# A third accumulator for the in-projection, from the scan's idle PSUM banks, and an earlier release of held-back loads

## The chip, the cores and the metric

One NeuronCore of a Trainium2 chip runs the whole kernel in one launch. The metric is the device time of a launch in microseconds, the median over several executions. The engines that matter are TensorE (PE in the rows), VectorE (DVE), ScalarE (ACT) and SyncE (SP), whose queue issues all the weight loads.

## What is computed

The block is a pre-norm hybrid decoder layer on 256 tokens of width 2048. Cut to what matters here:

```python
h = rms_norm(x, g1) * (1 + scale1) + shift1        # scale, shift, gate: columns of c @ w_mod
u, k, q, v, gates = split(h @ w_in)                # 2048 x 8192: 4 x 1024 columns and 2 x 2048
y_attn = moba_attention(rotary(norm(q)), rotary(norm(k)), v)
y_ssm  = s5_branch(u)                              # a diagonal scan over the 256 tokens
x = x + gate1 * (merge(y_attn, y_ssm, sigmoid(gates)) @ w_out)
x = x + gate2 * conv_ffn(rms_norm(x, g2) * (1 + scale2) + shift2)
```

## The kernel before

**Weights.** Every weight tile is 512 KB (128 partitions of 1024 floats). SP loads it into a ring of five `raw` buffers; ACT rounds it into `whi` (line 213, three buffers), DVE subtracts into `wlo` (line 218, three buffers), and PE makes three products, activations split the same way. A `raw` slot is free again when its `wlo` is made. Modulation weights go through the same ring: tiles of `w_m` go straight to PE as `modp` (line 491), and the `raw` slot is free when those four products are done; tiles of `w_g` go to DVE (line 529), which reduces them there. `load_ahead` issues loads in the order of a list, `order`, as far as the ring has room; modulation loads are held back in `behind_weights` until two more weight tiles have been issued (`LAG`).

**The first stage.** The in-projection is made in five chunks of its 16 k-tiles (2, 2, 4, 4, 4). In each chunk the blocks u (2), k (2), q (2), v (2) and one early gate block `gep` (two in chunk 0) each get a partial sum; in the last chunk the order is u, k, gates, q, v. Between chunks a partial sum lives in SBUF. So from chunk 1 on each block begins with a seed, an ACT copy from SBUF into the PSUM accumulator (line 287 for `up`, 366 for `kp`, `qp`, `vp`, four copies at line 285 for the gates), and ends with an ACT copy back (line 1079, or 1136 for gates) that is written one weight tile later. The accumulators alternate between two PSUM buffers of two banks each (`mm_tile`). Two more banks (`bu_tile`) are for the scan, which begins in the last chunk, when u is finished.

**Order.** The program is written in one order by the planner, and the tile framework schedules each engine's instructions from it; each engine then runs its own list in order, waiting for semaphores. Beside the projections, pieces of other work are woven in: the modulation of the next chunk, the scan's set-up, the scan itself (`zp`, `zt`, `kp` of `cpad`, `bu`, `py`), the norms and rotations of k and q, and transposes `qt`. After the chunks come the rest of the gates (`gsp`), the attention, the branch projections and the feed-forward part, which is some three quarters of the time.

Of the kernel before, what the change touches and what calls it, by code (L numbers as in the profile page):

```python
# [42 lines left out]
def block_kernel(ctx: ExitStack, tc: tile.TileContext, I, out):  # L43
# [11 lines left out]
    def mm_tile(shape, name):  # L55
        return ps.tile(shape, F32, name=name, tag="mm", bufs=2)
# [3 lines left out]

    def py_tile(shape, name):
        return ps.tile(shape, F32, name=name, tag="py", bufs=1)

    def m1_tile(shape, name):
        return ps.tile(shape, F32, name=name, tag="m1", bufs=1)
# [22 lines left out]
    def wsrc(w, kb, c0):  # L88
        return w[kb, c0 // 512]
# [15 lines left out]
    place = {"seen": 0}  # L105


    order, behind_weights = [], []
# [7 lines left out]
    def ring_of(i):  # L116
        return "mod" if plan[i][0] == "m" and "mod" in ring else "w"

    def see_next():

        i = place["seen"]
        place["seen"] += 1
        if plan[i][3] and ring_of(i) == "w":
            behind_weights.append([i, plan[i][3]])
            return
        order.append(i)
        if plan[i][0] == "w":
            for entry in behind_weights:
                entry[1] -= 1
            while behind_weights and behind_weights[0][1] <= 0:  # L130
                order.append(behind_weights.pop(0)[0])

    def load_next():
        i = order.pop(0)
        src = plan[i][1]
        r = ring_of(i)
        held[r] += 1
        raw = ring[r]()

        if r == "mod" and "lo" in place:  # L140
            V.tensor_copy(raw[:, 0, 0:1], place["lo"][:, 0, 0:1].bitcast(F32))
        flat = raw.rearrange("p a b -> p (a b)")
        DMA.dma_start(flat, src)
        loaded[i] = (raw, r)
# [9 lines left out]
    def follow(inst):  # L154
        if "mod" in behind:
            after(inst, behind.pop("mod"))
# [5 lines left out]
    def load_ahead():  # L162
        while True:
            while not order and place["seen"] < len(plan):
                see_next()
            if not order:
                break
            r = ring_of(order[0])
            if held[r] >= room[r]:
                break  # L170
            load_next()
# [14 lines left out]
    def later(n, fn):  # L186
        agenda.setdefault(clock["step"] + n, []).append(fn)
# [13 lines left out]
    def take_back(g):  # L201
        bg[:] = [entry for entry in bg if entry[0] is not g]

    def drain(g):
        for _ in g:
            pass
        take_back(g)
# [18 lines left out]
    def add_weights(src, fn):  # L226
        weights.append(len(plan))
        plan.append(("w", src, fn, 0))
# [38 lines left out]
    def chan_block(name, w, c0, kbs, act_hi, act_lo, post, k0=0, w0=None, seed=None, groups=None):  # L267

        st = {}

        def step(u, hi, lo):
            if u == 0:
                if groups:
                    st["m"] = []
                    for make, ms in zip((mm_tile, bu_tile, py_tile), groups):
                        part = make([128, len(ms), 256], name)
                        st["m"] += [part[:, i] for i in range(len(ms))]
                else:
                    st["p"] = mm_tile([128, 4, 256], name)
                    st["m"] = [st["p"][:, m] for m in range(4)]  # L280
                if seed is not None:
                    src = seed()
                    if isinstance(src, list):
                        for m in range(4):
                            A.copy(st["m"][m], src[m])
                    else:
                        A.copy(st["p"].rearrange("p a b -> p (a b)"), src)
            p = st["m"]
            starts = [ms[0] for ms in groups] if groups else (0, 2)
            for m in range(4):  # L290
                ms = slice(128 * m, 128 * m + 128)
                for k in range(2):
                    kk = k0 + 2 * u + k
                    first = u == 0 and k == 0 and seed is None
                    follow(PE.matmul(p[m], hi[:, k, ms], act_hi(kk), start=first and m in starts,
                                     stop=False, skip_group_check=True))
                    PE.matmul(p[m], hi[:, k, ms], act_lo(kk), start=False, stop=False,
                              skip_group_check=True)
                    PE.matmul(p[m], lo[:, k, ms], act_hi(kk), start=False,
                              stop=u == kbs - 1 and k == 1, skip_group_check=True)  # L300
                for ms in groups if groups and u == kbs - 1 else ():
                    if ms[-1] == m:
                        post(p, ms)
            if u == kbs - 1 and not groups:
                later(1, lambda: post(st["p"]))

        for u in range(kbs):
            add_weights(wsrc(w, (w0 if w0 is not None else k0 // 2) + u, c0),
                        lambda hi, lo, u=u: step(u, hi, lo))
# [48 lines left out]
    def tok_block(name, w, c0, kbs, act_hi, act_lo, post, k0=0, seed=None):  # L358

        st = {}  # L360

        def step(u, hi, lo):
            if u == 0:
                st["p"] = mm_tile([128, 2, 512], name)
                if seed is not None:
                    A.copy(st["p"], seed())
            p = st["p"]
            for k in range(2):
                kk = k0 + 2 * u + k
                for t in range(2):  # L370
                    ts = slice(128 * t, 128 * t + 128)
                    follow(PE.matmul(p[:, t], act_hi(kk)[:, ts], hi[:, k],
                                     start=u == 0 and k == 0 and seed is None, stop=False,
                                     skip_group_check=True))
                    PE.matmul(p[:, t], act_hi(kk)[:, ts], lo[:, k], start=False, stop=False,
                              skip_group_check=True)
                    PE.matmul(p[:, t], act_lo(kk)[:, ts], hi[:, k], start=False,
                              stop=(u == kbs - 1 and k == 1), skip_group_check=True)
            if u == kbs - 1:
                later(1, lambda: post(p))  # L380

        for u in range(kbs):
            add_weights(wsrc(w, k0 // 2 + u, c0), lambda hi, lo, u=u: step(u, hi, lo))
# [40 lines left out]
    for i in range(2):  # L424
        p = mm_tile([128, 2, 512], "cb")
# [611 lines left out]
    def all_mods():  # L1037
        while mods:
            next_mod()

    def parts_of(units):
        return sum(len(unit) for unit in units)
# [84 lines left out]
    def sig_post(b, p):  # L1127
        if b % 2 == 0:
            sig_s[b // 2] = e8("sig_s")
        A.activation(sig_s[b // 2][:, 4 * (b % 2):4 * (b % 2) + 4], p, AF.Sigmoid)  # L1130
# [6 lines left out]

    cols = {"u": 3072, "k": 1024, "q": 0, "v": 2048}
    last = len(chunks) - 1
    for c, (k0, nk) in enumerate(chunks):  # L1140
        place["mod"] = 0.0
        if c < last:
            mods += mod1(*chunks[c + 1])
            rate = parts_of(mods) / (4 * nk - 2.0 + nk // 2 * EARLY[c])
        else:
            drain(set_gen)
            mods += mod2(0)
            rate = R_LAST
        for key in "ukgqv" if c == last else "ukqvg":
            for b in range(2 if key != "g" else EARLY[c]):  # L1150
                def add():
                    if key == "g":
                        chan_block("gep", w_in, 6144 + 512 * b, nk // 2, h_hi, h_lo,
                                   lambda p, b=b, c=c: sig_post(b, p) if c == last else keep(b, p), k0=k0,
                                   seed=(lambda b=b: sums[b]) if c else None)
                        return
                    seeded = c > 0
                    (chan_block if key == "u" else tok_block)(
                        key + "p", w_in, cols[key] + 512 * b, nk // 2, h_hi, h_lo,
                        lambda p, key=key, b=b, c=c: gather(key, b, c, p, seeded), k0=k0,  # L1160
                        seed=(lambda key=key, b=b: part(key, b)) if seeded else None)

                with_mods(add, rate)
        all_mods()
        go()
# [278 lines left out]
```

## Time and the profile before

| | |
|---|---|
| median of 3 runs | 1524.7 us (1523.32 to 1530.68) |
| the profiled execution | 1520.47 us, of which 1518.6 us are the span of its instructions |
| mean granted TensorE clock in it | 0.987 of full speed |
| TensorE busy | 96% of the span |
| VectorE, ScalarE busy | 73%, 55% |

The profile gives for each instruction its start, its duration and, in brackets, how long its engine had stood idle before it and who ended that. Busy shares are averages over the whole span, so a single stage is read from a table by stretches of time and from the instructions themselves.

### The profile page before, as it was taken

The numbers are of one execution on the slowest core, as the hardware profiler recorded it, in microseconds if no ns is written. First come the engines' busy times: TensorE is split into PE (matmuls) and PEld (weight loads), VectorE is DVE, ScalarE is ACT, GpSimd is POOL, SyncE is SP. The second block draws the span as 40 slices with busy tenths as digits, with TensorE's granted clock in tenths as the row PEclk, the third lists the DMA queues.
The fourth block names the chain that finished last, engine by engine and source line by source line (L and its number), as shares of the span: only waits on it lengthen the run. The fifth ranks groups of instructions, "written<-read, shape, count | busy, mean of one in ns | idle before, by whom it ended". The sixth has DMA issues, their size and how long they took to land.

```text
span 1518.6 us, 24307 instructions
## 1 busy us (share of the span) xinstructions
PE 1463.7 (96%) x9382; PEld 1237.9 (82%) x9382; DVE 1109.5 (73%) x1881; ACT 842.0 (55%) x1193; POOL 9.8 (1%) x22
## 2 busy tenths in 40 slices
PE   7979999899999999999989999999999999999998
PEld 4657768689977788888868888888888888888887
DVE  3879865886677889998578888886555667766654
ACT  4755767867775534654445555555444455555443
POOL 1000000000000000000000000000000000000000
PEclk9989999999999999999999999999999999999999
DMA  8878888533458887978576777775555555555663
GB/s 322 306 238 307 304 321 296 179 126 126 139 170 298 300 301 276 332 262 315 176 281 235 245 263 262 246 258 191 194 189 188 193 190 186 193 191 186 205 212 107
DMA packets 99109, 353.47 MB, mean 233 GB/s; under 512 B 10961, under 2 KB 13137, under 8 KB 98993
## 3 DMA queue, kind: packets, MB, share of 16 engines
q1 hardware_dynamic: 97808, 348.17, 66.7%
q0 software_dynamic: 1040, 3.61, 0.7%
q8 instruction: 73, 1.20, 0.3%
q14 instruction: 42, 0.34, 0.1%
q10 hardware_dynamic: 146, 0.15, 0.0%
HBM read 349.79 MB, written 2.10 MB: 232 GB/s over the span
## 4 chain that ended last, share of the span: by engine, by line
PE 74%; DVE 10%; DMA 6%; ACT 5%; issue 3%; POOL 0%; SPq 0%; ACTq 0%; DVEq 0%
PE dp L329 11%; PE vp L329 10%; PE gp L329 10%; PE dp L331 6%; PE vp L331 5%; PE gp L331 5%; PE outp L329 4%; DVE wlo L218 4%; ACT whi L213 2%; PE outp L331 2%; PE modp L491 2%; PE ppp L329 2%; PE gap L329 2%; DMA raw<-in_w_m_dram 2%; DMA raw<-in_w_g_dram 2%
## 5 line engine op out<-in xcount | busy, mean ns | idle before, releaser
L218 DVE TENSOR_TENSOR wlo<-raw,whi 128x1024 fp32r<-128x1024 f32 x464 | 566.1, 1222 | 296.6 <-ACT whi L213 294.6
L213 ACT CAST whi<-raw 128x1024 fp32r<-128x1024 f32 x464 | 487.0, 1051 | 521.4 <-PE dp L329 131.8
L329 PE MATMUL vp<-hl,whi 128*128 128x512 f32 x704 | 244.9, 391 | 1.2 <-DVE gate L1307 1.2
L329 PE MATMUL dp<-g,whi 128*128 128x512 f32 x704 | 244.3, 391 | 0.0
L329 PE MATMUL gp<-hl,whi 128*128 128x512 f32 x640 | 222.3, 391 | 0.0
L331 PE MATMUL dp<-g,wlo 128*128 128x256 f32 x704 | 197.7, 281 | 0.0
L331 PE MATMUL vp<-hl,wlo 128*128 128x256 f32 x704 | 197.1, 280 | 0.0
L331 PE MATMUL gp<-hl,wlo 128*128 128x256 f32 x640 | 179.2, 280 | 0.0
L329 PEld LDWEIGHTS vp<-hl,whi 128*128 128x128 f32 x704 | 131.7, 187 | 30.5 <-ACT whi L213 1.5
L329 PEld LDWEIGHTS dp<-g,whi 128*128 128x128 f32 x704 | 131.9, 187 | 28.6
L329 PEld LDWEIGHTS gp<-hl,whi 128*128 128x128 f32 x640 | 119.7, 187 | 26.2
L331 PEld LDWEIGHTS vp<-hl,wlo 128*128 128x128 f32 x704 | 133.1, 189 | 0.0
L331 PEld LDWEIGHTS dp<-g,wlo 128*128 128x128 f32 x704 | 133.0, 189 | 0.0
L331 PEld LDWEIGHTS gp<-hl,wlo 128*128 128x128 f32 x640 | 121.0, 189 | 0.0
L329 PE MATMUL gap<-hl,whi 128*128 128x512 f32 x256 | 92.7, 403 | 0.0
L329 PE MATMUL outp<-m,whi 128*128 128x512 f32 x256 | 90.8, 399 | 0.0
L529 DVE SCALAR_TENSOR_TENSOR raw<-raw,cb 128x1024 f32<-128x1024 f32 x60 | 73.1, 1219 | 22.0 <-DMA raw<-in_w_g_dram 21.5
L529 DVE SCALAR_TENSOR_TENSOR mraw<-mraw,cb 128x1024 f32<-128x1024 f32 x56 | 68.2, 1221 | 17.4 <-DMA mraw<-in_w_g_dram 16.9
L331 PE MATMUL gap<-hl,wlo 128*128 128x256 f32 x256 | 72.2, 282 | 0.5 <-DVE wlo L218 0.5
L331 PE MATMUL outp<-m,wlo 128*128 128x256 f32 x256 | 71.4, 280 | 0.0
L329 PEld LDWEIGHTS gap<-hl,whi 128*128 128x128 f32 x256 | 48.0, 188 | 17.1 <-issue 3.4
L491 PE MATMUL modp<-raw,cpad 128*32 128x512 f32 (+1 forms) x320 | 53.9, 573 | 7.4 <-DMA raw<-in_w_m_dram 6.7
(343 smaller groups left out, 2597.7 us busy)
## 6 DMA issues: line engine op xcount, KB each, us to landing
raw<-in_w_up_dram SPq DMA_DIRECT2D x176, 512.0 KB, 3.6
raw<-in_w_in_dram SPq DMA_DIRECT2D x96, 512.0 KB, 4.8
raw<-in_w_down_dram SPq DMA_DIRECT2D x88, 512.0 KB, 3.5
raw<-in_w_m_dram SPq DMA_DIRECT2D x68, 512.0 KB, 5.1
raw<-in_w_g_dram SPq DMA_DIRECT2D x60, 512.0 KB, 5.1
mraw<-in_w_g_dram SPq DMA_DIRECT2D x56, 512.0 KB, 5.1
raw<-in_w_ga_dram SPq DMA_DIRECT2D x32, 512.0 KB, 4.5
raw<-in_w_out_dram SPq DMA_DIRECT2D x32, 512.0 KB, 4.2
```

Source lines behind the costliest of these rows:

```text
L213: A.copy(hi, loaded[i][0])
L218: V.tensor_sub(lo, loaded[i][0], hi_lo[i][0].bitcast(F32))
L329: follow(PE.matmul(joined(p[m]), hi4[:, k, ms], joined(a), start=u == 0 and k == 0, stop=False, skip_group_check=True))
L331: PE.matmul(p[m][:, 0], lo4[:, k, ms], a[:, 0], start=False, stop=u == kbs - 1 and k == 3, skip_group_check=True)
L491: mm = PE.matmul(st["p"][r0:r0 + 32], cpad[:, k], raw[:, i], start=k < 4, stop=k >= 12, tile_position=(0, r0))
L529: V.scalar_tensor_tensor(flat, flat, 1.0, cb[:, 1024 * half:1024 * half + 1024], op0=ALU.mult, op1=ALU.mult, accum_out=sums[:, k, half:hal ...
```

## The change

A counter, `place["acc"]`, runs while the chunks before the last are written. Each accumulator of a projection block counts it up, and every third one is taken from the scan's two banks instead of the alternating pair. When the last chunk is written the counter is deleted, and all is as before. In `load_ahead`, when nothing is left in the list of loads and a modulation load is still held back, that load is now put in the list.

```diff
+    def acc_tile(shape, name):
+        if "acc" not in place:
+            return mm_tile(shape, name)
+        place["acc"] += 1
+        return (bu_tile if place["acc"] % 3 == 0 else mm_tile)(shape, name)
...
     def load_ahead():
         while True:
             while not order and place["seen"] < len(plan):
                 see_next()
+            if not order and behind_weights:
+                order.append(behind_weights.pop(0)[0])
             if not order:
                 break
...
 def chan_block(...):
-                    st["p"] = mm_tile([128, 4, 256], name)
+                    st["p"] = acc_tile([128, 4, 256], name)
...
 def tok_block(...):
-                st["p"] = mm_tile([128, 2, 512], name)
+                st["p"] = acc_tile([128, 2, 512], name)
...
+    place["acc"] = 0
     for c, (k0, nk) in enumerate(chunks):
         place["mod"] = 0.0
         if c < last:
             mods += mod1(*chunks[c + 1])
             rate = parts_of(mods) / (4 * nk - 2.0 + nk // 2 * EARLY[c])
         else:
+            del place["acc"]
             drain(set_gen)
```

With the second edit alone no instruction of any engine changes its place or its waits. With the first alone the lists are those of the whole change. SP and POOL keep their order; only what SP's loads wait for changes. PE's list differs in a middle part, and its last 7066 instructions are the same; on the time axis of the profile before, all lists agree again from about 342 us on. Lines of the changed kernel are 9 higher (7 in `load_ahead`).

Two stretches of ScalarE's list in chunk 1, and one of SyncE's in the last chunk, show what moves. First ScalarE in the middle of chunk 1, before:

```order
L366 COPY kp<-k 128x1024
L455 ACTIVATE scr<-scr 128x128
L1079 COPY k<-kp 128x2x512
L213 CAST whi<-raw 128x1024
L366 COPY qp<-q 128x1024
L456 ACTIVATE scr<-scr 128x128
L1079 COPY k<-kp 128x2x512
L213 CAST whi<-raw 128x1024
L366 COPY qp<-q 128x1024
L1079 COPY q<-qp 128x2x512
L213 CAST whi<-raw 128x1024
L366 COPY vp<-v 128x1024
```

and with the change:

```order
L375 COPY qp<-q 128x1024
L464 ACTIVATE scr<-scr 128x128
L1088 COPY k<-kp 128x2x512
L222 CAST whi<-raw 128x1024
L375 COPY qp<-q 128x1024
L465 ACTIVATE scr<-scr 128x128
L1088 COPY k<-kp 128x2x512
L222 CAST whi<-raw 128x1024
L375 COPY vp<-v 128x1024
L1088 COPY q<-qp 128x2x512
L222 CAST whi<-raw 128x1024
L375 COPY vp<-v 128x1024
```

Each seed stands one block earlier (the first seed of q where the second of k stood), while the copies back and the casts keep their places. Second, ScalarE at the end of chunk 1, before:

```order
L1079 COPY v<-vp 128x2x512
L213 CAST whi<-raw 128x1024
L285 COPY gep<-gsum 128x256 x4
L498 COPY rows<-modp 128x512
L213 CAST whi<-raw 128x1024
L607 ACTIVATE hl<-t,sh_110 128x256 x4
L1079 COPY v<-vp 128x2x512
L213 CAST whi<-raw 128x1024 x2
L287 COPY up<-u 128x1024
```

and with the change:

```order
L1088 COPY v<-vp 128x2x512
L294 COPY gep<-gsum 128x256
L296 COPY up<-u 128x1024
L222 CAST whi<-raw 128x1024
L294 COPY gep<-gsum 128x256 x3
L507 COPY rows<-modp 128x512
L222 CAST whi<-raw 128x1024
L616 ACTIVATE hl<-t,sh_110 128x256 x4
L1088 COPY v<-vp 128x2x512
L222 CAST whi<-raw 128x1024 x2
```

The seed of chunk 2's first u block has moved up between the gate block's four seeds. Third, SyncE's queue in the last chunk, with the engine whose semaphore each load waits for (`DMAHW` is an earlier load), before:

```order
L143 DMA raw<-in_w_in_dram 128x1024 [waits DMAHW6_49,PE_49]
L143 DMA raw<-in_w_g_dram 128x1024 [waits DMAHW7_49,DMAHW4_49,PE_49]
L143 DMA raw<-in_w_in_dram 128x1024 [waits DMAHW1_49,DVE_49]
L143 DMA raw<-in_w_m_dram 128x1024 [waits DMAHW2_49,DVE_49]
L143 DMA raw<-in_w_m_dram 128x1024 [waits DMAHW6_49,PE_49]
L143 DMA raw<-in_w_g_dram 128x1024 [waits DMAHW0_49,DVE_49]
```

and with the change:

```order
L150 DMA raw<-in_w_in_dram 128x1024 [waits DVE_49]
L150 DMA raw<-in_w_g_dram 128x1024 [waits DMAHW6_49,DMAHW4_49,PE_49]
L150 DMA raw<-in_w_in_dram 128x1024 [waits DMAHW7_49,PE_49]
L150 DMA raw<-in_w_m_dram 128x1024 [waits DMAHW1_49,DVE_49]
L150 DMA raw<-in_w_m_dram 128x1024 [waits DMAHW2_49,DVE_49]
L150 DMA raw<-in_w_g_dram 128x1024 [waits DMAHW6_49,DMAHW0_49,PE_49]
```

The loads are the same in the same order, but the ring's slots come free one step differently: the two `w_m` loads now wait for the two `wlo` steps for which a `w_in` load and the first `w_m` load waited before, and the second `w_m` load no longer waits for PE's work on the first. The reason stands in DVE's list, where one step on a `w_g` tile has moved from behind the first part of the scan's arithmetic to ahead of it. Before, around the later place:

```order
L910 SCALAR_TENSOR_TENSOR r<-w,z_rot 128x2x256
L953 TENSOR_TENSOR k<-k,ta_1309 128x2x256
L912 TENSOR_TENSOR r<-w,z_rot 128x2x256
L954 TENSOR_TENSOR k<-k,qb 128x2x256
L914 TENSOR_TENSOR w<-w,z_rot 128x1024
L529 SCALAR_TENSOR_TENSOR raw,gsum<-raw,cb 128x1024
L218 TENSOR_TENSOR wlo<-raw,whi 128x1024
```

and with the change:

```order
L919 SCALAR_TENSOR_TENSOR r<-w,z_rot 128x2x256
L962 TENSOR_TENSOR k<-k,ta_1309 128x2x256
L921 TENSOR_TENSOR r<-w,z_rot 128x2x256
L963 TENSOR_TENSOR k<-k,qb 128x2x256
L923 TENSOR_TENSOR w<-w,z_rot 128x1024
L227 TENSOR_TENSOR wlo<-raw,whi 128x1024
```

The step at line 529 (538) is gone from here; it stands ahead of the scan's first product (`r<-bu`), some 35 rows up.

## Rows read from the trace of the kernel before

**Rows 1.** The page: busy time and share of each engine, whole span.
```profile
PE 1463.7 (96%) x9382; PEld 1237.9 (82%) x9382; DVE 1109.5 (73%) x1881; ACT 842.0 (55%) x1193; POOL 9.8 (1%) x22
```

**Rows 2.** Busy time by stretches (length, engines, granted clock, DMA share, GB/s).
```profile
60.00:111.00 51.00, 40.70 (x187) 26.27 (x185) 39.48 (x148) 31.93 (x45) 0.00 (x0) 0.90 0.74 258
111.00:169.00 58.00, 56.88 (x324) 45.27 (x325) 54.81 (x124) 38.34 (x47) 1.61 (x4) 1.00 0.89 309
231.00:316.00 85.00, 75.60 (x512) 58.80 (x510) 62.62 (x123) 69.22 (x167) 0.00 (x0) 0.92 0.67 228
600.00:1518.00 918.00, 906.16 (x5253) 789.73 (x5251) 656.41 (x946) 465.48 (x574) 2.84 (x4) 1.00 0.65 221
```

**Rows 3.** Waits of PE, 0 to 420 us (total, times, longest).
```profile
PE modp L491 <- DMA raw<-in_w_m_dram: 6.5, 7, 3.5
...
PE gep L295 <- ACT gep L285: 4.1, 2, 3.2
```

**Rows 4.** PE in chunk 1: start, duration, instruction, idle before and releaser.
```profile
75.19 0.50 PE L372 MATMUL qp<-whi,hl 128*128 128x512 f32 x1 [1.95 <-ACT qp L366]
...
86.94 0.79 PE L372 MATMUL vp<-whi,hl 128*128 128x512 f32 x1 [2.30 <-ACT vp L366]
...
99.82 0.39 PE L295 MATMUL gep<-hl,whi 128*128 128x256 f32 x1 [3.20 <-ACT gep L285]
...
111.47 0.39 PE L295 MATMUL up<-hl,whi 128*128 128x256 f32 x1 [2.54 <-ACT up L287]
```

**Rows 5.** ACT around the first and last of these waits.
```profile
72.26 1.01 ACT L1079 COPY k<-kp 128x1024 f32<-128x1024 f32 x1 [0.44 <-PE kp L377]
73.17 1.05 ACT L213 CAST whi<-raw 128x1024 fp32r<-128x1024 f32 x1
74.11 1.02 ACT L366 COPY qp<-q 128x1024 f32<-128x1024 f32 x1
...
108.52 1.99 ACT L213 CAST whi<-raw 128x1024 fp32r<-128x1024 f32 x2
110.42 1.00 ACT L287 COPY up<-u 128x1024 f32<-128x1024 f32 x1
```

**Rows 6.** Two stretches at the lower clock, columns as in the stretches above.
```profile
86.70:90.10 3.40, 3.15 (x8) 1.36 (x8) 2.99 (x15) 0.96 (x3) 0.00 (x0) 0.50 0.93 266
...
288.00:294.90 6.90, 5.58 (x29) 2.58 (x32) 5.77 (x10) 3.08 (x15) 0.00 (x0) 0.51 0.87 301
```

**Rows 7.** PE in the last chunk.
```profile
261.15 0.58 PE L295 MATMUL gep<-hl,whi 128*128 128x256 f32 x1 [0.91 <-ACT gep L285]
...
284.76 1.05 PE L491 MATMUL modp<-raw,cpad 128*32 128x512 f32 x4 [0.44 <-DMA raw<-in_w_m_dram]
289.32 1.92 PE L491 MATMUL modp<-raw,cpad 128*32 128x512 f32 x4 [3.51 <-DMA raw<-in_w_m_dram]
...
310.89 0.49 PE L851 MATMUL bu<-u,zt 64*128 64x128 f32 x2 [1.40 <-ACT zt L832]
...
316.20 0.58 PE L295 MATMUL gsp<-hl,whi 128*128 128x256 f32 x1
```

**Rows 8.** SP's queue in the last chunk: issues of loads.
```profile
278.78 0.33 SPq L143 DMA_DIRECT2D raw<-in_w_in_dram  x1
280.15 0.33 SPq L143 DMA_DIRECT2D raw<-in_w_m_dram  x1
...
285.85 0.33 SPq L143 DMA_DIRECT2D raw<-in_w_m_dram  x1
```

**Rows 9.** DVE in the last chunk: the step on a `w_g` tile.
```profile
285.45 1.22 DVE L529 SCALAR_TENSOR_TENSOR raw<-raw,cb 128x1024 f32<-128x1024 f32 x1
```

**Rows 10.** ACT in the last chunk, its idle times.
```profile
282.25 1.06 ACT L213 CAST whi<-raw 128x1024 fp32r<-128x1024 f32 x1 [0.92 <-DMA raw<-in_w_in_dram]
...
291.29 0.58 ACT L498 COPY rows<-modp 128x512 f32<-128x512 f32 x1 [2.05 <-PE modp L491]
...
294.68 0.65 ACT L968 COPY qkT<-qt 128x256 f32<-128x256 f32 x2 [1.64 <-PE qt L965]
```

## The prediction

> **What bounds the kernel now.** I read the page first: TensorE is busy for 1463.7 of 1518.6 us [rows 1], so only about 55 us of idle time are there for anyone to win. The table by stretches says where they are [rows 2]. From 600 us to the end PE works 906.16 of 918 us; nothing is to be had there. In chunk 1 (60 to 111 us) it works 40.70 of 51 us, in the last chunk (231 to 316 us) 75.60 of 85 us. Those two stretches hold 20 us of idle time, and both are ones that the change rearranges.
>
> The waits of PE say for what it stands idle [rows 3]: the loads of `w_m` cost 6.5 us in all, half of it in one wait of 3.5 us, and the gates' seeds 4.1 us. The timeline of chunk 1 then shows four waits, all put down to a seed [rows 4]: 1.95, 2.30, 3.20 and 2.54 us, 9.99 us together. In the last chunk the idle times are 0.91 us for a gate seed, 0.44 and 3.51 us for the two `w_m` tiles, 1.40 us for `zt` of the scan [rows 7]. Idle time costs twice: behind each long wait TensorE stands at the lower of its two clock levels (1.2 GHz), 3.40 us at 0.50 from 86.70 on, 6.90 us at 0.51 from 288.00 on [rows 6], and the same four modulation products take 1.92 us instead of 1.05 [rows 7].
>
> **The release of held-back loads.** Alone it moves no instruction and no wait on any engine. Its price is 0, and a gain or a loss is excluded, since every list stays the same.
>
> **The third accumulator in chunks 1 to 3.** It adds and removes no instruction; seeds only move one block ahead in ACT's list. The trace says why that may buy little. The seed of the waiting q block ran at 74.11, directly behind the cast at 73.17, and that one directly behind the copy back at 72.26, which itself waited for the last matmul of the k block [rows 5]. With the change the seed is done earlier, but the cast of the same block's weights keeps its place behind the copy back, and the first matmul needs both. The cast ended at 73.17 + 1.05 = 74.22 us and the seed at 75.13; the wait can shrink by 0.9 us, not by 1.95. In exchange four modulation products, which ran ahead of that wait, now stand behind it in PE's list: 1.05 us of work that used the wait are done afterwards. I price this block at 0, and the v block, where copy, cast and seed stand in the same order, likewise. In the gate block the order is even worse: between the first and the second of its four seeds there now stand a u seed of 1.0 us and a cast of 1.05 us. The first seed is earlier, the others later. I take 0 again, with bounds of -3.2 us (the wait gone) and +2.1 us (both copies in the wait).
>
> The last of the four waits is better. The first u block of chunk 2 waited at 111.47 for a seed that ACT made at 110.42, behind two casts that ended at 108.52 + 1.99 = 110.51 [rows 4, 5]. That seed is now made in chunk 1. The cast of the block's first tile ends half way through those two, at about 109.5 us, and the matching `wlo`, which takes 1.22 us as the DVE step of the same tile size does [rows 9], follows it; so the block can begin near 110.2 us, a gain of 1.3 us. Chunk 2 is fed just in time: the DMA engines are busy for 0.89 of it, at 309 GB/s [rows 2]. What starts earlier there soon waits for its weights. I let half of the 1.3 us survive: **-0.7 us**, between 0 and -1.3.
>
> **What the skill says of it.** The Trainium skill, TensorE: Matmul & The Clock Gate, section Architectural detail, says that ScalarE and VectorE take their instructions strictly in order. By that rule the accumulators were never what held the seeds up, and the sum for the three waits is the 0 above; without it a free bank would release the seeds at once, and the three waits of 1.95, 2.30 and 3.20 us would go, 7.45 us. The trace agrees with the rule in the one place shown: the cast came directly behind the copy that waited 0.44 us, and the seed directly behind the cast.
>
> **The gate block of the last chunk.** It waits 0.91 us for its fourth seed [rows 7], which stands behind scan copies on ACT. With the freer accumulators three of those seeds and the scan pieces are woven differently, and the block begins directly behind the scan's first pieces. I take the whole wait: **-0.9 us**, between 0 and -2.6, if the half-speed time behind it (about 3.4 us, half of it lost) goes too.
>
> **The second `w_m` load.** This is the largest term, and a side effect. A step on a `w_g` tile ran at 285.45 on DVE [rows 9], far behind its data, because it stood behind the scan's first arithmetic; it held a `raw` slot all that time. Now it stands ahead of the scan, the slot comes free early, and each later load takes over the slot of its predecessor. The first `w_m` load is then released by the `wlo` that released a `w_in` load at 278.78, the second by the one that released the first at 280.15, instead of by PE's work on the first tile at 285.85 [rows 8]. That is 5.70 us earlier. From issue to use the first load took 284.76 - 280.15 = 4.6 us; the second is thus there at about 284.8, or 283.9 with the 0.9 us of the gate block. PE ends the first tile's products about then, does the second's in 1.05 us at full clock instead of 1.92, and is done near 285.5 instead of 289.32 + 1.92 = 291.24: 5.7 us earlier, the 0.9 us included.
>
> How much of it arrives at 316 us? The next work on PE is chained to ACT, which is nearly full there: 69.22 of 85 us in this stage [rows 2]. ACT can move ahead only by its own idle times: 0.92 us for a `w_in` load (which is issued earlier too), 2.05 us for the modulation products and 1.64 us for a transposed k, 4.6 us together [rows 10], plus the 0.9 us of the gate block, 5.5 us. PE itself would gain more (the 1.40 us for `zt` and some of the half-speed time [rows 6, 7]), but it waits for ACT. The smaller number decides: the gates' block `gsp` that begins at 316.20 [rows 7] begins **5.5 us** earlier, of which the gate block above is 0.9. The lower bound of the gain is that 0.9 alone, if ACT can't use the time; the upper one is 5.7 + 1.9 (half of the 3.7 us at half speed between 291.2 and 294.9 [rows 6]) + 1.40 = 9.0 us.
>
> **Behind that.** From about 342 us on all lists are the same, and PE is busy for 99% of the long rest [rows 2], so what is won at 316 us stands at the end.
>
> **The sum.** -0.7 - 5.5 = -6.2 us. The profiled execution would go from 1520.47 to 1514.3. It lies 4.2 us below the median of the runs; taken off the median, 1524.7 - 6.2 = **1518.5 us**. About 0.5% (7.6 us) is what a measurement of this kernel can tell from no change, so this forecast lies inside that bound, near its edge.
>
> **Rivals.**
> *The gain stays in the last chunk.* ACT is 81% busy there; if it runs its norm and rotation steps ahead of the copy that releases PE, or if the `w_m` tiles land later because more loads are under way at once, `gsp` begins at most 1 to 2 us earlier. For it: PE, ACT and DVE hand work to each other in short steps there. Against: ACT stood idle for 2.05 us precisely for the modulation products. Time: 1524.7 - 1.5 = 1523.2 us.
>
> *The waits of chunk 1 go after all, and the clock stays up.* If each of the three blocks gains the 0.9 us by which the seed trailed the cast, and the full 1.3 us at 111 us survives, that is 4.0 us; with one or two of the stretches at half speed gone (3.40 us each [rows 6], half of it lost, 1.7 us) about 6.5 us, and with 5.5 us from the last chunk 12 us: 1512.7 us. For it: each stretch of low clock follows a wait. Against: the casts stay behind the copies back. The same page of the Trainium skill (section What's actually happening) says that the lower clock is the default and that activity releases it; the rows of both stretches fit that, and by it shorter waits would help twice.
>
> *Slower: chunk 1 delays the loads.* The modulation products stand behind longer waits, the gate block's later seeds come behind a u seed and a cast, so PE gives back `w_m` slots later; SP issues in order, and everything behind such a load is late in a stage that has no slack (0.89 DMA share [rows 2]). Price: up to 2.1 us in the gate block, 1 us of modulation work behind each of two waits, and a further 1.7 us at half speed, 5.8 us in all. That cancels the 5.5 us of the last chunk; it becomes a loss only if those fail to arrive as well. Then the time is about 1524.7 + 5 = 1529.7 us. It decides from the point where chunk 4 starts more than 5.5 us later than the 231 us of now.
>
> *It does nothing it is meant to do*: for the release edit that is certain, for the accumulator it is the first rival.
>
> **Chances.** Forecast (-3.5 to -9 us) 0.42, gain lost in the last chunk 0.22, larger gain 0.26, slower 0.10. Faster by over 0.5%: nearly all of the larger gain and a third of the forecast, 0.41. Slower by over 0.5%: part of the last rival, 0.06. Within 0.5%: the rest, 0.53. The range runs from 1509 (-15.7 us, beyond the middle of the larger gain) to 1525.5 (the lost gain included), and leaves out a few per cent below and most of the slower case.
>
> **What would show it.** Right: the second `w_m` load issued near 279 to 280 us and no wait of over 1 us for it; `gsp` starting near 310 us; ACT's idle time before the `rows` copy gone; the q, v and gate blocks of chunk 1 still waiting 2 to 3.5 us each, now put down to the cast; the first u block of chunk 2 starting near 110 us. Wrong: chunk 2 starting later than 111.47 us, or `gsp` not before 315 us (loss), or chunk 1 without waits of over 1 us (larger gain).

## The result, and the profile after

The changed kernel takes 1511.8 us, the median of 9 runs (1506.1 to 1520.5), against 1523.3 us for 9 runs of the kernel before (1513.1 to 1530.7). The medians lie 11.5 us apart. The estimate used below is the ratio of the two kernels' runs, 0.9943, with a 95% interval of 0.992 to 0.9966: 8.7 us less, between 5.2 and 12.2. The forecast was 6.2 us less, 1518.5 us, with a range of 1509 to 1525.5.

The profiled execution of the changed kernel is the longest of its nine, 1520.5 us, and its span happens to equal the one of before, 1518.6 us. So the spans say nothing; stages have to be compared. The table by stretches, columns as in [rows 2]:

```profile
60.00:111.00 51.00, 40.91 (x187) 25.74 (x186) 37.33 (x145) 30.24 (x46) 0.00 (x0) 0.90 0.75 258
111.00:169.00 58.00, 57.42 (x320) 44.73 (x319) 56.02 (x116) 40.05 (x49) 0.00 (x0) 1.00 0.86 306
231.00:316.00 85.00, 78.30 (x566) 63.14 (x566) 67.55 (x138) 70.18 (x170) 0.00 (x0) 0.94 0.64 224
600.00:1518.00 918.00, 904.95 (x5219) 785.85 (x5217) 651.89 (x936) 462.48 (x571) 2.84 (x4) 1.00 0.64 220
```

Chunk 1 is as idle as it was (40.91 against 40.70 us of 51 us [rows 2]); the last chunk has 2.7 us more PE work in the same 85 us. The waits of PE in the first 420 us, as in [rows 3]:

```profile
...
PE gep L304 <- ACT gep L294: 3.5, 1, 3.5
PE bu L860 <- ACT zt L841: 3.2, 2, 1.8
PE vp L381 <- ACT whi L222: 2.8, 1, 2.8
PE modp L500 <- DMA raw<-in_w_m_dram: 2.3, 2, 1.6
PE qp L384 <- DVE wlo L227: 2.1, 1, 2.1
...
PE qp L381 <- ACT whi L222: 2.0, 1, 2.0
```

The waits for `w_m` loads fell from 6.5 to 2.3 us. The q and v blocks wait as long as before or a little longer, now for the cast instead of the seed. One wait has grown, that of a q block of the last chunk for `wlo`: 2.1 us where it was 1.2. The places of [rows 4] in the timeline of PE:

```profile
76.18 0.49 PE L381 MATMUL qp<-whi,hl 128*128 128x512 f32 x1 [2.05 <-ACT whi L222]
...
88.63 0.50 PE L381 MATMUL vp<-whi,hl 128*128 128x512 f32 x1 [2.81 <-ACT whi L222]
...
102.72 0.39 PE L304 MATMUL gep<-hl,whi 128*128 128x256 f32 x1 [3.45 <-ACT gep L294]
...
111.63 0.28 PE L304 MATMUL up<-hl,whi 128*128 128x256 f32 x1
...
112.54 0.39 PE L308 MATMUL up<-hl,wlo 128*128 128x256 f32 x1 [0.51 <-DVE wlo L227]
```

And those of [rows 7], with SP's issues for [rows 8]:

```profile
256.46 0.39 PE L304 MATMUL gep<-hl,whi 128*128 128x256 f32 x1
...
281.91 1.07 PE L500 MATMUL modp<-raw,cpad 128*32 128x512 f32 x8
...
301.19 0.49 PE L860 MATMUL bu<-u,zt 64*128 64x128 f32 x2 [1.76 <-ACT zt L841]
...
309.47 0.39 PE L304 MATMUL gsp<-hl,whi 128*128 128x256 f32 x1
```

```profile
275.12 1.70 SPq L150 DMA_DIRECT2D raw<-in_w_m_dram  x2
```

The two `w_m` loads are issued back to back, their eight products run in one piece at full clock, and no wait stands ahead of them. `gsp` begins at 309.47 us instead of 316.20.

For the comparison of kernels I measure stages between named instructions of PE's timeline, so that one execution's early luck doesn't move the later ones. *Chunk 1* is from the first `up` matmul of chunk 1 to that of chunk 2. The last chunk is from its first `up` matmul to its first gate matmul (*gate*), on to the end of the last modulation products (*mod*), to the first `gsp` matmul (*gsp*), and to the first score `sc` of the attention (*score*). All in us, one profiled execution each:

| kernel | chunk 1 | gate | mod | gsp | score | last chunk |
|---|---|---|---|---|---|---|
| before | 50.4 | 29.7 | 30.1 | 25.0 | 11.6 | 96.3 |
| changed | 50.1 | 26.6 | 26.5 | 26.5 | 9.9 | 89.5 |
| zp late | 50.8 | 27.3 | 26.8 | 24.9 | 9.9 | 88.9 |
| late w_g | 45.8 | 26.8 | 30.4 | 23.3 | 10.0 | 90.5 |
| changed, in turn | 41.0 | 28.2 | 26.8 | 26.4 | 9.9 | 91.2 |
| accumulator only | 49.9 | 27.3 | 26.8 | 26.6 | 9.9 | 90.6 |
| before, in turn | 43.9 | 28.1 | 29.3 | 25.3 | 11.7 | 94.4 |
| in turn, zp late | 42.4 | 27.0 | 28.0 | 25.0 | 9.9 | 89.9 |
| release only | 48.1 | 28.7 | 28.4 | 24.9 | 11.7 | 93.6 |
| in turn, late w_g | 40.3 | 26.3 | 31.3 | 23.3 | 10.0 | 90.8 |

### The profile page after: what moved, and what is told of

Read it like the earlier page. It is cut to its first block, busy times and chain, and to the rows that moved or that the text cites. A ratio compares the mean times of both kernels' runs of the same rounds, so it can differ in the third digit from the quotient of the medians.

```text
span 1518.6 us, 24309 instructions
## 1 busy us (share of the span) xinstructions
PE 1466.5 (97%) x9382; PEld 1238.1 (82%) x9382; DVE 1109.9 (73%) x1881; ACT 840.9 (55%) x1193; POOL 9.8 (1%) x22
## 4 chain that ended last, share of the span: by engine, by line
PE 77%; DVE 8%; DMA 6%; ACT 5%; issue 3%; SPq 0%; POOL 0%; DVEq 0%; ACTq 0%
PE vp L338 11%; PE dp L338 11%; PE gp L338 10%; PE dp L340 6%; PE vp L340 6%; PE gp L340 5%; PE outp L338 3%; DVE wlo L227 3%; PE gap L338 2%; PE modp L500 2%; ACT whi L222 2%; PE ppp L338 2%; PE outp L340 2%; DMA raw<-in_w_in_dram 2%; DMA raw<-in_w_m_dram 1%
## 5 line engine op out<-in xcount | busy, mean ns | idle before, releaser
L222 ACT CAST whi<-raw 128x1024 fp32r<-128x1024 f32 x464 | 486.8, 1050 | 523.5 <-PE dp L338 131.8
L338 PE MATMUL vp<-hl,whi 128*128 128x512 f32 x704 | 248.7, 397 | 2.2 <-DVE gate L1318 2.2
L338 PEld LDWEIGHTS dp<-g,whi 128*128 128x128 f32 x704 | 131.9, 187 | 28.7
L338 PEld LDWEIGHTS gp<-hl,whi 128*128 128x128 f32 x640 | 120.0, 187 | 28.1
L338 PE MATMUL outp<-m,whi 128*128 128x512 f32 x256 | 90.8, 399 | 0.1
L338 PEld LDWEIGHTS outp<-m,whi 128*128 128x128 f32 x256 | 48.0, 188 | 14.3 <-issue 2.9
```

The costliest lines, as they stand in the source:

```text
L222: A.copy(hi, loaded[i][0])
L338: follow(PE.matmul(joined(p[m]), hi4[:, k, ms], joined(a), start=u == 0 and k == 0, stop=False, skip_group_check=True))
```

## The experiments

**The last chunk's order without the accumulator (zp late).** The kernel before, plus an edge that only orders: the scan's first transposes may not stand ahead of the last matmul that was written before them.

```diff
-                PE.transpose(zp[:, j], bflat[:, j // 2, j % 2], ident)
+                tp = PE.transpose(zp[:, j], bflat[:, j // 2, j % 2], ident)
+                if ct == 0:
+                    after(tp, behind["blk"])     # the last matmul of a tok_block
```

> The kernel before, with two PSUM accumulators as it had, and one edit: the four transposes (zp) with which the scan begins may not run ahead of the last written matmul of the projections. That alone gives every engine the order of the last chunk that the whole change gives it. If the gain lies in the last chunk's order, this run gains nearly all of it without a third accumulator: 6 to 8 us below the kernel before, ratio 0.995 to 0.996, the gates' block gsp starting near 309 to 311 us, and the second w_m tile not waited for. If the gain comes from the third accumulator in chunks 0 to 3, the time is that of the kernel before within 2 us.

Ratio 0.9966 (0.9939 to 0.9992), 5.2 us less, a little short of the 6 to 8 us expected. The last chunk takes 88.9 us, as with the whole change; chunk 1 takes 50.8 us, as before. So the last chunk's gain needs no third accumulator. The accumulator in chunks 0 to 3 only led the scheduler to put the four transposes together in the last chunk, where before two of them stood in chunk 3.

**The `w_g` step put back (late w_g).** The whole change, with the sixth DVE step of that gate block ordered behind the scan's first product of `w` and `z_rot`.

```diff
+            if part == 3 and (k0, k, half) == (0, 2, 1):
+                after(wg, place["scan0"])        # w<-w,z_rot of the first scan step
```

> The whole change, with one step on a w_g tile on DVE put back behind the first part of the scan's arithmetic, where the kernel before had it; the slot of its tile is freed late again and the second w_m load waits for PE's work on the first once more. If the early second load is a term of its own, as the prediction has it, PE waits 3 to 4 us for the second w_m tile again, and about 4 us of the gain are gone: ratio 0.996 to 0.998. If the loads are hidden behind ACT's work, the time is that of the whole change (0.994) within 1.5 us.

Ratio 0.9958 (0.9936 to 0.9981). It falls between the two expectations, and the accumulator alone, which has the lists of the whole change, came to 0.9954 against the same runs of the kernel before: no loss that the times can tell. The wait is back in full, in PE's timeline:

```profile
282.98 1.92 PE L500 MATMUL modp<-raw,cpad 128*32 128x512 f32 x4 [3.54 <-DMA raw<-in_w_m_dram]
```

It costs 3.9 us up to the last modulation products (30.4 against 26.5 us), but the next piece is 3.2 us shorter (23.3 against 26.5). The table by stretches for exactly that piece, of before, of the whole change and of this run:

```profile
291.24:316.20 24.96, 22.87 (x181) 17.36 (x180) 20.61 (x55) 22.67 (x68) 0.00 (x0) 0.84 0.62 201
```

```profile
282.98:309.47 26.49, 22.77 (x192) 17.52 (x192) 24.22 (x59) 24.74 (x71) 0.00 (x0) 0.87 0.62 219
```

```profile
284.90:308.24 23.34, 22.09 (x192) 17.00 (x191) 19.37 (x51) 21.42 (x63) 0.00 (x0) 0.92 0.55 189
```

ACT, whose busy time is the fourth in the row, is busy for 91 to 93% in all three, and with the early load it has 71 instructions to do in the piece instead of 63. The stretches ahead of these pieces, from the first gate matmul to the end of the last modulation products, show the other side. First the whole change, then this run:

```profile
256.46:282.98 26.52, 23.89 (x153) 18.62 (x147) 22.56 (x47) 23.35 (x59) 0.00 (x0) 0.94 0.56 197
```

```profile
254.52:284.90 30.38, 24.54 (x153) 17.82 (x147) 25.69 (x51) 26.35 (x66) 0.00 (x0) 0.95 0.57 194
```

With the late load ACT does 3.0 us more there. ACT's list moved with the load: this edge changes PE's, DVE's and ACT's lists, not only the place of one step. In this run a copy back of q, the copy `dec`, a seed of v and two of the sixteen steps that sum the squares of q (`junk`) stand ahead of the `rows` copy that takes up the products:

```profile
279.39 0.99 ACT L1091 COPY q<-qp 128x1024 f32<-128x1024 f32 x1
280.28 0.61 ACT L893 COPY dec<-z_m 128x504 f32<-128x504 f32 x1
280.80 1.01 ACT L375 COPY vp<-v 128x1024 f32<-128x1024 f32 x1
281.74 0.31 ACT L951 ACTIVATE junk<-q 128x128 f32<-128x128 f32 x1
...
284.95 0.58 ACT L507 COPY rows<-modp 128x512 f32<-128x512 f32 x1 [2.38 <-PE modp L500]
```

In the whole change all of them stand behind it:

```profile
283.07 0.58 ACT L507 COPY rows<-modp 128x512 f32<-128x512 f32 x1 [0.61 <-PE modp L500]
283.55 1.02 ACT L1088 COPY q<-qp 128x1024 f32<-128x1024 f32 x1
...
284.98 0.34 ACT L948 ACTIVATE junk<-q 128x128 f32<-128x128 f32 x1
...
285.29 1.04 ACT L375 COPY vp<-v 128x1024 f32<-128x1024 f32 x1
...
287.06 0.64 ACT L891 COPY dec<-z_m 128x504 f32<-128x504 f32 x1
```

What ACT does while PE waits for the load, it has to do later when PE doesn't wait.

**Blocks in turn (changed, in turn).** The whole change, with an edge that keeps PE's projection blocks in written order in chunks 0 to 3.

```diff
+    def in_turn(inst, first):
+        if first and "turn" in place and "blk" in behind:
+            after(inst, behind["blk"])           # the last matmul of the block before
...
+                    in_turn(mm, m == 0 and k == 0)
```

> The whole change, with PE's matmuls of the projection blocks kept in the order in which they are written in chunks 0 to 3 (no matmul of a later block ahead of a block that is ready). If the waits of 2.05, 2.81 and 3.45 us that chunk 1 has with the change come from that order, as a first matmul standing ahead of a ready block, they shrink to under 1 us each and chunk 2 begins 3 to 7 us earlier: ratio to the kernel before 0.990 to 0.992. If chunk 1 is held by ACT's in-order copies and casts or by the loads, the waits move to other blocks, chunk 2 begins within 1.5 us of 111.6 us, and the ratio stays at 0.994.

Ratio 0.9924 (0.9896 to 0.9952). Chunk 1 takes 41.0 instead of 50.1 us, a larger gain than expected. In PE's timeline the waits for cast and seed are gone; what is left are `w_m` loads:

```profile
74.07 1.05 PE L508 MATMUL modp<-raw,cpad 128*32 128x512 f32 x4 [1.05 <-DMA raw<-in_w_m_dram]
...
84.34 1.05 PE L508 MATMUL modp<-raw,cpad 128*32 128x512 f32 x4 [2.31 <-DMA raw<-in_w_m_dram]
...
94.32 1.05 PE L508 MATMUL modp<-raw,cpad 128*32 128x512 f32 x4 [2.00 <-DMA raw<-in_w_m_dram]
```

The waits of [rows 4] came from PE's own list. It put the first matmul of the q block, which needs a late cast and a late seed, ahead of the whole second k block. In the whole change that k block's seed, `whi` and `wlo` were made by 72.08 us, but its first matmul ran at 80.76 us, behind the wait that ended at 76.18:

```profile
66.56 1.02 ACT L375 COPY kp<-k 128x1024 f32<-128x1024 f32 x1
...
68.53 1.05 ACT L222 CAST whi<-raw 128x1024 fp32r<-128x1024 f32 x1 [0.95 <-DVE scr L456]
...
70.86 1.22 DVE L227 TENSOR_TENSOR wlo<-raw,whi 128x1024 fp32r<-128x1024 f32 x1
...
80.76 0.50 PE L381 MATMUL kp<-whi,hl 128*128 128x512 f32 x1
```

The same holds for v and the gates, where the block behind became ready 1.2 and 0.5 us into the wait. PE runs its list in order, so some 2.9 us of ready work, the twelve matmuls of a block, stood behind each of those. Chunk 1 from its first `up` matmul to that of chunk 2, with the whole change and in turn:

```profile
61.58:111.63 50.05, 40.16 (x181) 25.19 (x182) 36.38 (x144) 29.29 (x43) 0.00 (x0) 0.90 0.74 257
```

```profile
61.76:102.75 40.99, 34.76 (x181) 23.59 (x182) 36.06 (x143) 29.64 (x43) 0.00 (x0) 1.00 0.90 312
```

PE is idle for 3.7 us less (9.9 against 6.2), and its same 181 matmuls are busy for 5.4 us less, at a granted clock of 1.00 instead of 0.90. The time of the kernel gains less than the stage: 0.9924 against 0.9943 is about 3 us, the intervals overlap, and where the rest of the 9 us goes is not shown.

**The accumulator alone.** The two lines in `load_ahead` are left out.

> The third accumulator without the earlier release of held-back loads. Every engine's order is that of the whole change. If the release edit is worth nothing, the ratio is that of the whole change, 0.992 to 0.9966. If the release brings the gain, it is 1.000. It also tells how far two profiles of one order differ behind 342 us, where all lists agree.

Ratio 0.9954 (0.993 to 0.9979), stages as with the whole change.

**The release alone.** Only those two lines.

> The release of held-back loads alone. Order and waits of every engine are those of the kernel before, so the ratio is 1.000 within 0.0025, and the stages take what they took before: chunk 1 about 50 us, last chunk about 96 us. If the release moved loads after all, the last chunk would be shorter by 1 us or more. It also shows how far two series of one and the same order differ.

Ratio 1.0006 (0.9984 to 1.0027). Its stages show the spread of one order: 48.1 and 50.4 us for chunk 1, 93.6 and 96.3 us for the last chunk.

**In turn, without the accumulator (before, in turn).** The edge of the third experiment in the kernel before.

> The kernel before, without the third accumulator, with PE's projection blocks kept in their written order in chunks 0 to 3; the last chunk keeps the order of the kernel before. If chunk 1 was held by PE's list alone, it takes about 41 us as with the whole change in that order (41.0 us, against 50.4 us before), and the time falls by 8 to 10 us: ratio 0.994. If the third accumulator is needed for it, since seeds must wait for one of two banks pairs to be copied out, chunk 1 still takes 45 us or more and the ratio is above 0.996.

Ratio 0.9966 (0.9946 to 0.9987), on the side of the second expectation; chunk 1 takes 43.9 us, between the two. Here the edge changes almost nothing but the places of the q, v and gate matmuls in PE's list, so the 6.5 us of chunk 1 are the order's. The last chunk stays long, 94.4 us.

**Both edges, without the accumulator (in turn, zp late).**

> The kernel before, without the third accumulator, with both order edges: the projection blocks in written order in chunks 0 to 3, and the scan's first transposes not ahead of the projections. If the third accumulator matters only through the orders that it leads to, this equals the whole change with kept order: ratio 0.992, chunk 1 about 41 us, last chunk (from its first u block to the first score) about 90 us against 96.3 us before. If the accumulator is worth time of its own, it stays 2 us or more behind: ratio 0.994 or above.

Ratio 0.9931 (0.9906 to 0.9955), last chunk 89.9 us, chunk 1 42.4 us. Beside the 0.9924 of the whole change in turn that is no difference that the times can tell. In chunk 1 the two kernels without the accumulator need 43.9 and 42.4 us, the two with it 41.0 and 40.3 us. That the third bank saves 1 to 4 us there with the blocks in turn is thus possible but not shown: chunk 1 of one and the same order differs by as much between executions (48.1 and 50.4 us above).

**Both together with the late step (in turn, late w_g).**

> The whole change with the projection blocks in written order, and the step on the w_g tile put back behind the scan's arithmetic. A second look at the second w_m load: if its early issue is made back by ACT's work behind it, as in the run with that edit alone, PE waits 3 to 4 us more for the w_m tile, the piece from there to gsp is about 3 us shorter, the last chunk takes 90 to 91 us as without the edit, and the ratio stays near 0.992. If it is a term of its own, the last chunk takes 94 us and the ratio is 0.995.

Ratio 0.9917 (0.9893 to 0.9941). The late load again costs 4.5 us (31.3 against 26.8), again 3.1 us come back (23.3 against 26.4), and the last chunk takes 90.8 us, 0.4 us less than with the early load.

**Without the norm of q.** Two kernels leave out the sixteen ACT steps that sum the squares of q and set the sums to a constant, one with the early load, one with the late one.

```diff
+        if i == 0:
+            V.memset(s16, 128.0)
-        for t in range(2):
+        for t in range(2 * i):
             for h in range(8):
                 A.activation(junk, r4[:, t, h], AF.Square, accum_out=s16[:, t, h:h + 1])
```

> The whole change without the sixteen ACT steps that sum the squares of q (the sums are set to a constant, so q is not normalised): about 7 us of ACT work less behind the last modulation products. If ACT's fullness there (24.7 of 26.5 us busy) is what sets the start of gsp and of the first score, the piece from the last modulation products to the first score, 36.4 us with the whole change, falls by 3 to 6 us. If PE or the loads set it, it falls by under 1 us.

> The same with the step on the w_g tile put back behind the scan's arithmetic, so that the second w_m load is late by some 4 us again. With those ACT steps in place the late load costs 3.9 us up to the last modulation products and gives about 3 us back behind them. If that is because ACT does the q steps while PE waits, then without them less is given back, and the last chunk up to the first score takes 3 to 4 us longer than in the run without the q steps and with the early load; if the cause is another, the difference is again about 1 us.

From the last modulation products to the first score it takes 33.7 us with the early load (16.7 + 17.1), 2.6 us less than the 36.4 us of the whole change: less than expected, but ACT's work does set part of the pace. Only this sum can be compared, because PE's list changes too: the last 32 `bu` matmuls, which stand ahead of the first `gsp` block in the whole change, stand behind it here. With the late load the products end 5.2 us later in the last chunk (32.0 us behind its first gate matmul against 26.8), and behind them 1.6 us come back (32.1 against 33.7 us), where 3.0 us come back with the q steps. The last chunk takes 87.1 us with the early load and 90.4 us with the late one, a difference of 3.3 us; with the q steps it was 1.0 us in one pair and -0.4 us in the other. So less comes back without the q steps, and the difference is the one that the first expectation for the late kernel names. Its reason, that ACT does the q steps while PE waits, holds for two of the sixteen only, as shown above; and part of the difference is that the load itself cost more. Each of the two is one execution, so how much of it the q steps account for stays open. The wait of ACT for the products in the run with the late load, 270 to 320 us:

```profile
ACT rows L507 <- PE modp L500: 4.2, 1, 4.2
```

With the q steps in place ACT lost 2.4 us at this wait; here the two squares that stood ahead of it are gone, and PE's products come later.

**Earlier modulation loads in chunk 1.** The fastest version, with `LAG` 1 instead of 2 for these loads.

> The fastest version so far (written order of the projection blocks, late w_g step) with the modulation loads of chunk 1 held back by one weight tile instead of two, so that they are issued earlier. PE waits about 5.5 us for them there with the written order. If the waits are set by how late these loads stand in SP's queue, chunk 1 falls from 40.3 to 37 us or less and the ratio from 0.992 to 0.990. If the stage is bound by the DMA engines, the waits move to the weight tiles and chunk 1 stays at 40 us.

Chunk 1 takes 41.4 us and the ratio is 0.9937 (0.9912 to 0.9961). PE waits for no `w_m` load there any more; in its table of waits for 60 to 115 us stand others:

```profile
PE qp L392 <- DVE wlo L231: 2.3, 1, 2.3
PE vp L387 <- ACT whi L226: 2.0, 1, 2.0
PE gep L314 <- DVE wlo L231: 1.0, 1, 1.0
```

The waits moved from one kind of tile to the other, as the second expectation said. That fits a stage held by its loads, but the run doesn't show the DMA engines themselves at their limit.

## Why the prediction was right, and where its steps were not

**The release of held-back loads, 0.** Right: 1.0006 alone, and the gain without it.

**The three waits of chunk 1, 0.** Right in size and in the sign of each: 2.05, 2.81 and 3.45 us against 1.95, 2.30 and 3.20 us [rows 4], the first two now put down to the cast, as forecast. The reason was only half of it. The prediction saw ACT's order of copies, casts and seeds; it saw that PE's list had moved modulation products behind the waits, but not that the waiting matmul itself stood ahead of a ready block. The lists showed it, and that order was worth 9 us of chunk 1 with the third bank (in turn) and 6.5 us without it (before, in turn).

**The first u block of chunk 2, -0.7.** The wait of 2.54 us for the seed is gone (0.51 us for `wlo` remain; the prediction's 110.2 us left out that this `wlo` ends 1.2 us behind its cast, near 110.7), but chunk 1 gave the time back: the block began at 111.63 us, 0.16 us later than before. Chunk 1 took 45.8 to 50.1 us in the three runs with this order of chunk 1 in the table and 48.1 to 50.8 us in those with the order of before, so neither a gain nor a loss of 0.7 us can be told here.

**The gate block, -0.9.** Right in kind, too small. It starts 26.3 to 28.2 us into the last chunk where the order is the new one, and 28.1 to 29.7 us where it is the old one: about 1.8 us by the means. Besides the seed the prediction should have counted the two short waits for `zt` ahead of the gate block, since with the four transposes together the copies come earlier.

**The second `w_m` load, the larger part of -5.5.** Right at its place, wrong in what it is worth. Both loads are issued 1.4 us apart, the second is waited for no longer, and the products end 3.9 us earlier in the stage than with the late step. The failed step is "ACT can move ahead only by its own idle times ... 4.6 us together". The sum took ACT's list as fixed and its idle times as gaps that close. But the work between them moved: with the late load ACT copies q back, copies `dec`, seeds v and sums two squares of q ahead of the `rows` copy, 3.0 us of work; with the early load the same work stands behind it, where ACT is 93% busy and is again the pace. The two runs with the late step put the load's worth at 3.9 and 4.5 us at its place, and at 1.0 and -0.4 us at the first score. Without the q steps it is 3.3 us, in one execution each. That was the outcome of the first rival, for this term, but not by its way: the `rows` copy was not held up by norm steps, it ran at 283.07 us, straight behind the products.

**What took its place.** The last chunk as a whole did gain what was forecast: by the means of the executions 94.8 us in three runs with the old order (93.6 to 96.3), 90.0 us in five with the new one and the early load (88.9 to 91.2), 4.8 us, against 5.5. In the two runs with the late step it is still 90.7 us. So most of the gain, about 4 us, is there without the early load, and goes with the order of the scan's pieces: about 2 us up to the gate block, the rest behind the modulation products. There sixteen more of the scan's `bu` matmuls run ahead of the first `gsp` block instead of behind it, ten more in the runs with the late step. How the latter splits between order and clock stays open: the piece that holds them ran at a mean granted clock of 0.84 and 0.85 in the kernels with the old order and 0.87 to 0.93 in the others, and each has one execution. No run has the early load with the scan's old order, so what it would be worth there is not shown. That the forecast's sum came out near the measured time is thus in part luck: the load was priced about 4 us too high, and the scan's order, which was hardly priced, brought about as much.

**Behind 342 us.** Right that the orders agree, and that nothing of it is lost to the order. But one execution doesn't carry the gain through unchanged (next section but one). Up to the first score the changed kernel is 9.9 us ahead of before, counted from the first matmul of chunk 0; the one with the accumulator alone, with the same lists, is 6.7 us ahead. But the release alone, with the lists of before, is 4.3 us ahead as well, so single executions don't fix the gain. The three kernels with the new order of the last chunk and without the edge in chunk 1 measured 5.2, 7.0 and 8.7 us (0.9966, 0.9954, 0.9943), with intervals that overlap.

**Rivals.** "The gain stays in the last chunk" was wrong as a whole and right for the load. "The waits of chunk 1 go after all" did not happen with this change; it happens with one more edge, for another reason than the seeds. "Slower" did not occur: chunk 4 began at 229.9 us, not behind 231. With the blocks in turn the clock did stay up: the whole of chunk 1 is at a granted clock of 1.00, the higher of the two levels (2.4 GHz), where it was 0.90 (the two rows of that experiment). The Trainium skill says (TensorE: Matmul & The Clock Gate, What's actually happening) that the lower clock is the default and that activity releases it. The run agrees: its longest wait there is 2.31 us instead of 3.45, and no stretch of chunk 1 is at the lower level. But the prediction's "behind each long wait" says too much. No stretch of low clock follows the waits of 2.31 and 2.00 us in this run; before, one followed the waits of 1.95 and 2.30 us, and none the wait of 2.54 us at 111.47 (1.00 from 111 to 169 us [rows 2, 4]). The length of a single wait doesn't settle it.

**The fastest versions measured.** The whole change with its blocks in turn: 0.9924 (0.9896 to 0.9952), or 0.9917 (0.9893 to 0.9941) with the late step, which can't be told apart. Against the whole change, 0.9943 (0.992 to 0.9966), the intervals overlap, so the times don't show that they are faster than the whole change. Chunk 1 does show the edge: it takes 40.3 to 43.9 us in every run that has it and 45.8 to 50.8 us in every run of the table that has not.

## What to carry to other kernels

When a wait is put down to a buffer, look at what stands behind the waiting instruction on its own engine: a list in which ready work waits behind one late instruction is mended by an order edge; here a third bank left the three waits as they were. Time won ahead of an engine that is 90% busy is only worth what that engine doesn't have to make up for, so count the instructions that it did during the wait, not only the length of the wait. And when a scheduler makes the order, a small edit can change it far from the edit; an edge that makes the same order without the edit tells which of the two was worth the time.

## What the runs showed of the hardware that was not expected

Between about 816 and 1050 us, where PE is busy without a gap and all kernels have the same list, executions run at one of two rates, both at a granted clock of 1.00. The rows by line of the same group, 816 to 1048 us, before and after:

```profile
L329 PE MATMUL gp<-hl,whi 128*128 128x512 f32 x320 | 111.2, 391 | 0.0
```

```profile
L338 PE MATMUL gp<-hl,whi 128*128 128x512 f32 x320 | 113.3, 399 | 0.0
```

399 ns instead of 391 for a matmul of 512 columns. From the 201st to the 801st matmul that writes `gp` (828 to 1021 us) the execution of before took 192.8 us and that of the changed kernel 196.5; over the whole stretch that makes about 4.4 us, an estimate from these two. Of the thirteen profiles eight are at the faster rate (192.7 or 192.8 us) and five at the slower one (196.4 or 196.5 us: the changed kernel, its version in turn, the kernel before in turn, one without the q steps and the one with earlier loads); the kernel with the accumulator alone, with the same lists as the whole change, is among the faster. What sets it stays open. The execution of the changed kernel also has two stretches at a lower mean clock, 500 to 525 us (0.93) and 800 to 820 us (0.91), where that of before has 1.00; the pieces of the list that hold them took 2.3 and 2.7 us longer.
